# Products of the delta rule's key tiles between the steps of the first projection tile's chain

## The chip, the cores and the metric

The kernel runs on one core of a Trainium2 chip. The metric is the time of one execution in microseconds on the device; before the change it is 2277.63 us, the median of 3 runs (2274.01 to 2280.87).

## What is computed

A trunk of two layers over 512 latent and 256 context tokens of width 1024. In each layer one normalised input goes through one combined input projection into three groups of heads: latent attention (MLA), a bidirectional gated delta rule (GDN) and a bidirectional gated linear attention (GLA). A gated convolutional FFN follows. The part that matters here is the projection and what is made of it for GDN and GLA, shortened from the reference:

```
parts = split(h @ w_in)           # cq, ckv, k_rope, gdn qkv, gate, a, b, gla q, k, v, gate, low rank
k_rope = apply_axial_rope(parts[2])
qkv = silu(dwconv_centred(parts[3], w_conv))       # q, k, v of the delta rule
g = -exp(A_log) * softplus(a + dt_bias); beta = sigmoid(b)
la = logsigmoid(low_rank @ w_gk + b_gk) / 16       # forget gates of GLA, both directions
q, k = l2norm(q), l2norm(k)
o, S = gated_delta_chunked(q, k, v, g, beta, S0)
```

## The kernel before, in words

Activations are kept feature-major: 8 tiles of 128 features by 768 tokens, context first. For accuracy every float32 operand of a projection is split into two fp32r parts, the activations into `hh` and `hl` (`prenorm`, L543 to L550: DVE, ACT and POOL), the weights into `wh` (a cast on ACT, L191) and `wl` (a subtraction on DVE, L192). `wsplit` loads a weight tile with one DMA (L200, into one of 3 `wr` buffers that the conditioning weights of `ada`, L476, use too) and splits its two halves of 4 feature tiles each; there are 3 buffers of `wh` and 3 of `wl`. One projection tile, 128 output features, is 48 products in `fsteps` (L212 through `mm`): 2 segments of 512 and 256 tokens by 8 feature tiles by 3 products (`hh` x `wl`, `hl` x `wh`, `hh` x `wh`), and it yields after each three, 16 times. The result is in a PSUM tile `bb`, of which there are two; smaller PSUM tiles are `a`, `b`, `c` and `d`.

`project_in` runs in each layer right behind the normalisation (in the last layer five kinds of tile come ahead). Its tile 0 holds the small features: the key's rotary part, the low-rank gate inputs, a and b of the delta rule. `misc` makes of them a chain:

- DVE multiplies the tile with the rope table `cse` into `misc` (L584; the table's DMA is L583);
- `selkr` sums the rotary halves on PE, ACT copies the result (L588), a DMA stores `krope` (L589);
- for each of two directions a product with `wgk` into a `bb` tile; DVE makes `m` (L600), ACT makes Abs (L601), Exp (L602) and Ln (L603) of it in `e`, POOL subtracts (L604), and a DMA stores `e` (L606);
- `gdn_gates`: six transposes of `misc` (L215), ACT's softplus and exponentials (L745 to L768), cumulated decays by products with `gg` and `gm`.

`gdn(0)` then makes the two key tiles of the delta rule, `gdn(2)` the two query tiles: each a projection tile, then `conv_silu` (copies `u` out of PSUM, L822, POOL and DVE taps into `cy`, silu on ACT, L808), transposes of `cy` into tokens-major `ktok` (L629), and sums of squares. `self.bg` holds the conditioning products of later stages, `ada`: one piece is issued by `tick` after each projection tile. `gdn_prep` and `gdn_scan` follow, with further projection tiles as their fill.

The code is written as generators. What is issued in the program's order is then ordered anew for each engine by the framework's scheduler, which allots the buffers as well; each engine carries out its instructions in the order that comes of this, and SP's queue issues the DMAs in order.

Of the kernel before, what the change touches and what calls it, by code (L numbers as in the profile page):

```python
# [44 lines left out]
HS, HG, HA, HM, HP = 0, 0, 0, 0, 0  # L45
EP = (1, 1)
WO = ((4, 5, 6, 7, 0, 1, 2, 3), (4, 5, 6, 7, 0, 1, 2, 3))
SPF = 0
XT = (2, 0, 1, 0, 1, 0, 1, 0)
LM = 2  # L50
MOB = 1
HB = 14
NS = 2
# [74 lines left out]
def drain(g):  # L128
    try:
        while True:  # L130
            next(g)
    except StopIteration as e:
        return e.value


class Net:
# [416 lines left out]
    def project_in(self, later):  # L553
# [5 lines left out]
        def fmt(i, segs=XC):  # L559
            wh, wl = self.wsplit(w[i])  # L560
            ps = self.bb()
            yield from self.fsteps(ps, wh, wl, self.hh, self.hl, segs, KT)
            self.tick(1)
            return ps
# [10 lines left out]
        def tok(pool, tag):  # L575
            return pool.tile([128, 6, 256], F32, name=self.nm(tag), tag=tag)

        def misc():

            ps = drain(fmt(0))  # L580
            self.misc = self.kt(name="misc")
            cse = self.kt(name="cse")
            nc.sync.dma_start(cse[:, :T], self.a["rope"][0])  # L583
            nc.vector.tensor_tensor(self.misc[:, :T], ps[:, 256:], cse[:, :T], op=ALU.mult)  # L584
            ps = self.bb()
            for a, b in XC:
                self.mm(ps[:, 256 + a:256 + b], self.c("selkr"), self.misc[:, a:b], True, True)
            nc.scalar.copy(cse[:, :T], ps[:, 256:])  # L588
            nc.sync.dma_start(self.krope, cse[:, :T])  # L589
            if SPF:  # L590
                self.gdn_gates()

            self.spd = []
            for d in range(2):
                ps = self.bb()
                for a, b in XC:
                    self.mm(ps[:, 256 + a:256 + b], self.wgk[:, d * 128:(d + 1) * 128], self.misc[0:32, a:b], True, True)
                e, m = self.kt(name="e")[:, :T], self.kt(name="m")[:, :T]
                bias = self.fm(P_BGK + d)
                nc.vector.tensor_scalar(m, ps[:, 256:], bias, 0.0, op0=ALU.add, op1=ALU.min)  # L600
                nc.scalar.activation(e, ps[:, 256:], AF.Abs, bias=bias)  # L601
                nc.scalar.activation(e, e, AF.Exp, scale=-1.0)  # L602
                nc.scalar.activation(e, e, AF.Ln, bias=1.0)  # L603
                nc.gpsimd.tensor_tensor(e, e, m, op=ALU.subtract)  # L604
                self.spd.append(self.dram([128, T], f"sp{d}"))
                nc.sync.dma_start(self.spd[d], e)  # L606
            if not SPF:
                self.gdn_gates()

        Gp, self.G = self.pool("G", "right")  # L610
        self.ktok, self.vtok, qtok = tok(self.F, "ktok"), tok(self.F, "vtok"), tok(self.G, "qtok")
# [4 lines left out]
        def gdn(m):  # L616
            dst = dsts[m]
            for i in range(2):
                segs = [XS] if (last and m == 2) else XC
                ps = yield from fmt(1 + 2 * m + i, segs)  # L620
                y = self.conv_silu(ps, P_CW + 3 * (2 * m + i), segs)
                for a, b in segs:
                    nt, t0 = (b - a) // 128, a // 128
                    pt = self.ab()
                    for t in range(nt):
                        c = a + t * 128 + (2 if a else 0)
                        self.transpose(pt[:, t * 128:(t + 1) * 128], y[:, c:c + 128])
                    pv = pt[:, :nt * 128].rearrange("p (t c) -> p t c", c=128)
                    nc.scalar.copy(dst[:, t0:t0 + nt, i * 128:(i + 1) * 128], pv)  # L629
                    if m != 1:  # L630
                        sq = self.F2.tile([128, 512], F32, name=self.nm("sq"), tag="sq", bufs=2)
                        sqv = sq[:, :nt * 128]
                        nc.scalar.activation(sqv, pt[:, :nt * 128], AF.Square)
                        nc.vector.reduce_sum(ssv[:, m // 2, t0:t0 + nt, 2 * i:2 * i + 2],
                                             sqv.rearrange("p (t h d) -> p t h d", h=2, d=64), axis=AX)
# [64 lines left out]
        if last:  # L700
            for g in (gdn(2), gate(0), gla_kq(1), mla_in(1)):
                drain(g)
        misc()
        if LM == 0:
            self.bg += later
        drain(gdn(0))
        if LM == 2:
            self.bg += later
        if not last:
            drain(gdn(2))  # L710
        self.tags = "a"
# [854 lines left out]
```

## Time and profile before

| | |
|---|---|
| median of 3 runs | 2277.63 us (2274.01 to 2280.87) |
| the profiled execution | 2278.35 us |
| its span | 2276.6 us |
| mean granted clock of TensorE | 0.934 |
| PE busy | 2045.0 us, 90% of the span |
| DVE, ACT, POOL busy | 1310.4, 1008.7, 536.0 us |
| DMA | 235.64 MB, 30.7% of 16 engines |

PE is matrix products, DVE VectorE, ACT ScalarE, POOL GpSimd, SP the engine that issues most DMAs. The granted clock is a share of TensorE's full 2.4 GHz; 0.5 is 1.2 GHz. A timeline row gives start, duration, engine, line, instruction, and in brackets how long the engine stood idle before it and what ended that. Products of PE overlap, so the distance between two starts is the price of one, not the duration. A row may stand for several instructions of the program: a float32 product counts as two.

### The profile page before, as it was taken

The numbers are of one execution on the slowest core, as the hardware profiler recorded it, in microseconds if no ns is written. First come the engines' busy times: TensorE is split into PE (matmuls) and PEld (weight loads), VectorE is DVE, ScalarE is ACT, GpSimd is POOL, SyncE is SP. The second block draws the span as 40 slices with busy tenths as digits, with TensorE's granted clock in tenths as the row PEclk, the third lists the DMA queues.
The fourth block names the chain that finished last, engine by engine and source line by source line (L and its number), as shares of the span: only waits on it lengthen the run. The fifth ranks groups of instructions, "written<-read, shape, count | busy, mean of one in ns | idle before, by whom it ended". The sixth has DMA issues, their size and how long they took to land. (4 is left out here: it accounts for less than half of the span.)

```text
span 2276.6 us, 44601 instructions
## 1 busy us (share of the span) xinstructions
PE 2045.0 (90%) x18168; PEld 1672.8 (73%) x18168; DVE 1310.4 (58%) x2474; ACT 1008.7 (44%) x1928; POOL 536.0 (24%) x897
## 2 busy tenths in 40 slices
PE   7898999888888799999999969988988777999996
PEld 4677777765667578888888857876766567888886
DVE  3354535668845743354454686556667757655556
ACT  4553323565464633332232456633446446543333
POOL 1342121135502310000010143413122613211102
PEclk8799999998898999999999979999989988999997
DMA  6232345422042354422212333111412053323322
GB/s 262 67 118 100 109 148 164 143 66 68 13 149 92 121 179 167 157 103 65 66 57 66 102 109 124 61 44 62 155 43 96 6 171 102 111 94 96 99 94 92
DMA packets 85134, 235.64 MB, mean 104 GB/s; under 512 B 9088, under 2 KB 24896, under 8 KB 84928
## 3 DMA queue, kind: packets, MB, share of 16 engines
q1 hardware_dynamic: 84928, 232.78, 30.7%
q8 instruction: 143, 2.34, 0.4%
q14 instruction: 63, 0.52, 0.1%
HBM read 204.04 MB, written 28.70 MB: 102 GB/s over the span
## 5 line engine op out<-in xcount | busy, mean ns | idle before, releaser
L212 PE MATMUL bb<-hh,wl 128*128 128x512 f32 (+1 forms) x1520 | 548.3, 361 | 18.0 <-DVE wl L192 10.9
L212 PE MATMUL bb<-hl,wh 128*128 128x512 f32 (+1 forms) x1520 | 542.0, 357 | 5.8 <-POOL hl L550 4.4
L192 DVE TENSOR_TENSOR wl<-wr,wh 128x512 fp32r<-128x512 f32 (+2 forms) x452 | 338.3, 751 | 362.3 <-ACT wh L191 361.0
L212 PE MATMUL bb<-hh,wh 128*128 128x512 f32 (+1 forms) x1520 | 540.2, 355 | 0.0
L191 ACT CAST wh<-wr 128x512 fp32r<-128x512 f32 (+2 forms) x452 | 274.1, 611 | 518.0 <-PE bb L212 370.3
L212 PEld LDWEIGHTS bb<-hh,wl 128*128 128x128 f32 x1520 | 293.2, 193 | 75.2 <-DVE wl L192 14.0
L212 PEld LDWEIGHTS bb<-hl,wh 128*128 128x128 f32 x1520 | 292.8, 193 | 49.4 <-POOL hl L550 7.8
L212 PEld LDWEIGHTS bb<-hh,wh 128*128 128x128 f32 x1520 | 292.9, 193 | 39.6 <-issue 2.1
L212 PE MATMUL bb<-g,wh 128*128 128x512 f32 (+1 forms) x1024 | 263.7, 349 | 2.3 <-DVE g L192 2.3
L1441 POOL TENSOR_SCALAR y<-u,fmt 128x512 f32<-128x512 f32 (+2 forms) x88 | 80.6, 917 | 527.1 <-ACT u L824 525.6
L212 PEld LDWEIGHTS bb<-g,wh 128*128 128x128 f32 x1024 | 181.5, 195 | 27.5 <-DVE g L192 3.3
L212 PE MATMUL bb<-g,wl 128*128 128x512 f32 (+1 forms) x512 | 180.3, 354 | 21.4 <-DVE wl L192 8.5
L212 PEld LDWEIGHTS bb<-g,wl 128*128 128x128 f32 x512 | 99.2, 195 | 36.9 <-ACT g L191 9.3
L824 ACT ACTIVATE u<-bb,fmt 128x512 f32<-128x512 f32 (+1 forms) x118 | 69.0, 613 | 85.0 <-PE bb L212 85.0
L212 PE MATMUL bb<-mh,wl 128*128 128x256 f32 (+1 forms) x256 | 85.2, 333 | 23.4 <-DVE wl L192 15.5
L1468 DVE TENSOR_TENSOR y<-y,bb 128x512 f32<-128x512 f32 (+2 forms) x80 | 54.8, 686 | 82.3 <-PE bb L212 82.2
L505 POOL TENSOR_TENSOR acc<-acc,sq 128x256 f32<-128x256 f32 (+1 forms) x48 | 49.5, 1031 | 183.9 <-ACT sq L503 180.9
L1442 DVE SCALAR_TENSOR_TENSOR y<-u,fmt,y 128x512 f32<-128x512 f32 (+2 forms) x88 | 72.3, 822 | 29.6 <-POOL y L1441 29.6
L212 PE MATMUL bb<-ml,wh 128*128 128x256 f32 (+1 forms) x256 | 84.1, 329 | 0.3
L1380 ACT ACTIVATE P<-bb,ast,srq 128x768 f32<-128x768 f32 (+1 forms) x80 | 72.6, 908 | 23.4 <-DVE ast L1378 14.5
L212 PE MATMUL bb<-mh,wh 128*128 128x256 f32 (+1 forms) x256 | 82.9, 324 | 0.0
L1377 DVE TENSOR_REDUCE ast<-bb 128x1 f32<-128x768 f32 (+1 forms) x80 | 67.2, 842 | 15.9 <-PE bb L212 15.6
(519 smaller groups left out, 3680.4 us busy)
## 6 DMA issues: line engine op xcount, KB each, us to landing
wr<-in_ffn_w_in SPq DMA_DIRECT2D x92, 512.0 KB, 3.5
wr<-in_w_ada SPq DMA_DIRECT2D x80, 512.0 KB, 3.9
wr<-in_ffn_w_out SPq DMA_DIRECT2D x48, 512.0 KB, 3.5
wr<-in_w_in SPq DMA_DIRECT2D x40, 512.0 KB, 4.3
wr<-in_w_out SPq DMA_DIRECT2D x32, 512.0 KB, 3.5
aw<-in_w_ada SPq DMA_DIRECT2D x16, 512.0 KB, 8.5
x<-in_xT SPq DMA_DIRECT2D x16, 384.0 KB, 8.7
wr<-in_w_uq SPq DMA_DIRECT2D x16, 192.0 KB, 2.6
```

The costliest lines, as they stand in the source:

```text
L191: self.nc.scalar.copy(hi, src)
L192: (eng or self.nc.vector).tensor_tensor(lo, src, hi.bitcast(F32), op=ALU.subtract)
L212: self.nc.tensor.matmul(out, l, r, start=start, stop=stop)
L505: (nc.vector, nc.gpsimd)[k % 2].tensor_tensor(acc[k % 2], acc[k % 2], sq, op=ALU.add)
L824: nc.scalar.activation(u[:, a + o:b + o], ps[:, off + a:off + b], AF.Identity, bias=bias)
L1377: nc.vector.reduce_max(st[:, 0:1], sc, axis=AX)
L1380: nc.scalar.activation(P[:, :w], sc, AF.Exp, bias=st[:, 0:1], scale=self.srq[:, t:t + 1], accum_out=st[:, 1:2])
L1441: nc.gpsimd.tensor_scalar(yv, u[:, lo + 1:lo + 1 + n], cw[1], self.fm(P_FCB + i), op0=ALU.mult, op1=ALU.add)
L1442: nc.vector.scalar_tensor_tensor(yv, u[:, lo:lo + n], cw[0], yv, op0=ALU.mult, op1=ALU.add)
L1468: nc.vector.tensor_tensor(y, y, p, op=ALU.add)
```

## The change

`misc` takes the generator of `gdn(0)`, and calls it twice. The first call, between the rope multiply and `selkr`, takes 16 steps: the products of the first key tile. The second, after `krope`'s store, takes 16 more: the rest of the first key tile (convolution, transposes, squares) and the products of the second. What is left of `gdn(0)` is drained after `misc`. The two constants that chose other places for `gdn_gates` and for `self.bg` go, with the places the same as before. Against the lines before, those between the constants and `misc` stand two lower in number (L210 for L212), those in `misc` two or three higher (L603 for L601), those behind it one lower (L807 for L808).

```diff
@@ -45,9 +45,7 @@
 HS, HG, HA, HM, HP = 0, 0, 0, 0, 0
 EP = (1, 1)
 WO = ((4, 5, 6, 7, 0, 1, 2, 3), (4, 5, 6, 7, 0, 1, 2, 3))
-SPF = 0
 XT = (2, 0, 1, 0, 1, 0, 1, 0)
-LM = 2
 MOB = 1
 HB = 14
 NS = 2
@@ -575,20 +573,24 @@
         def tok(pool, tag):
             return pool.tile([128, 6, 256], F32, name=self.nm(tag), tag=tag)
 
-        def misc():
+        def misc(beside):
+
+            def step():
+                for _ in range(16):
+                    next(beside)
 
             ps = drain(fmt(0))
             self.misc = self.kt(name="misc")
             cse = self.kt(name="cse")
             nc.sync.dma_start(cse[:, :T], self.a["rope"][0])
             nc.vector.tensor_tensor(self.misc[:, :T], ps[:, 256:], cse[:, :T], op=ALU.mult)
+            step()
             ps = self.bb()
             for a, b in XC:
                 self.mm(ps[:, 256 + a:256 + b], self.c("selkr"), self.misc[:, a:b], True, True)
             nc.scalar.copy(cse[:, :T], ps[:, 256:])
             nc.sync.dma_start(self.krope, cse[:, :T])
-            if SPF:
-                self.gdn_gates()
+            step()
 
             self.spd = []
             for d in range(2):
@@ -604,8 +606,7 @@
                 nc.gpsimd.tensor_tensor(e, e, m, op=ALU.subtract)
                 self.spd.append(self.dram([128, T], f"sp{d}"))
                 nc.sync.dma_start(self.spd[d], e)
-            if not SPF:
-                self.gdn_gates()
+            self.gdn_gates()
 
         Gp, self.G = self.pool("G", "right")
         self.ktok, self.vtok, qtok = tok(self.F, "ktok"), tok(self.F, "vtok"), tok(self.G, "qtok")
@@ -700,12 +701,10 @@
         if last:
             for g in (gdn(2), gate(0), gla_kq(1), mla_in(1)):
                 drain(g)
-        misc()
-        if LM == 0:
-            self.bg += later
-        drain(gdn(0))
-        if LM == 2:
-            self.bg += later
+        g0 = gdn(0)
+        misc(g0)
+        drain(g0)
+        self.bg += later
         if not last:
             drain(gdn(2))
         self.tags = "a"
```

How the change moves the instructions is shown at three places of layer 0. In the names, a number marks the buffer's turn: before, `bb_471` is the first projection tile, `bb_524` `selkr`, `bb_529` and `bb_541` the two `wgk` products, `bb_638` the first key tile; `a_554` and `b_559` are transposes of `misc`. PE before, from the end of the first tile:

```order
L212 MATMUL bb_471<-hl_93,wh_467 128x256
L212 MATMUL bb_471<-hh_85,wh_467 128x256
L212 MATMUL bb_524<-misc_520,cst 128x512
L212 MATMUL bb_524<-misc_520,cst 128x256
L212 MATMUL bb_529<-misc_520,wgk_212 128x512
L212 MATMUL bb_529<-misc_520,wgk_212 128x256
L215 MATMUL a_554<-cst,misc_520 128x128 x3
L215 MATMUL b_559<-cst,misc_520 128x128 x3
L212 MATMUL bb_541<-misc_520,wgk_212 128x512
L212 MATMUL bb_541<-misc_520,wgk_212 128x256
L212 MATMUL bb_638<-hh_78,wl_631 128x512
L212 MATMUL bb_638<-hl_86,wh_630 128x512
```

PE after the change, at the end of the first tile (`bb_534` is the first key tile, `bb_583` `selkr`, `bb_625` the second key tile):

```order
L210 MATMUL bb_534<-hh_80,wh_526 128x256
L210 MATMUL bb_534<-hh_81,wl_527 128x256
L210 MATMUL bb_471<-hl_93,wh_467 128x256
L210 MATMUL bb_471<-hh_85,wh_467 128x256
L210 MATMUL bb_534<-hl_89,wh_526 128x256
L210 MATMUL bb_534<-hh_81,wh_526 128x256
L210 MATMUL bb_534<-hh_82,wl_531 128x256
```

and further on, to the second key tile:

```order
L210 MATMUL bb_534<-hl_93,wh_530 128x256
L210 MATMUL bb_534<-hh_85,wh_530 128x256
L210 MATMUL bb_583<-misc_520,cst 128x512
L210 MATMUL bb_583<-misc_520,cst 128x256
L213 MATMUL c_699<-cst,misc_520 128x128 x3
L213 MATMUL d_704<-cst,misc_520 128x128 x3
L210 MATMUL bb_625<-hh_78,wl_618 128x512
```

The first key tile's products now stand among those of the first tile, its last 14 between that tile's end and `selkr`, and the second key tile follows the transposes of `misc`. Further on, PE after the change from the end of the second key tile (`bb_674` and `bb_686` are the two `wgk` products, `a_724` and `b_768` products of the gates, `a_863` conditioning products, `bb_810` the first query tile):

```order
L210 MATMUL bb_625<-hh_85,wh_621 128x256
L210 MATMUL bb_674<-misc_520,wgk_212 128x512
L210 MATMUL bb_674<-misc_520,wgk_212 128x256
L210 MATMUL a_724<-gg_711,cst 128x6x4 x2
L210 MATMUL a_724<-gg_711,cst 128x48
L210 MATMUL b_768<-gm_765,ones 64x48 x2
L210 MATMUL a_863<-wr_859,cTs 32x256 x4
L210 MATMUL a_863<-wr_861,cTs 32x256 x4
L210 MATMUL bb_686<-misc_520,wgk_212 128x512
L210 MATMUL bb_686<-misc_520,wgk_212 128x256
L210 MATMUL a_863<-cst,part_872 128x2 x2
L210 MATMUL bb_810<-hh_78,wl_803 128x512
```

Both `wgk` products, which stood ahead of the first key tile, now stand behind the second, with gate and conditioning products between them, and the third projection tile `bb_810` follows. ACT before, from the first table load of the gates (`e_532`, `e_544` are the two directions' gates):

```order
L753 ACT_TABLE_LOAD
L753 ACTIVATE gb_575<-abt_553 128x48
L601 ACTIVATE e_532<-bb_529,fmt_208 128x768
L745 ACTIVATE ge_565<-gz_564 128x48
L602 ACTIVATE e_532<-e_532 128x768
L746 ACTIVATE ge_565<-ge_565 128x48
L603 ACT_TABLE_LOAD
L603 ACTIVATE e_532<-e_532 128x768
L601 ACTIVATE e_544<-bb_541,fmt_208 128x768
L747 ACTIVATE ge_565<-ge_565 128x48
L602 ACT_TABLE_LOAD
L602 ACTIVATE e_544<-e_544 128x768
```

ACT after the change, from the cast of the third tile's second weights (`e_677`, `e_689` the two gates; `wr_904` are weights of the second query tile):

```order
L189 CAST wh_806<-wr_800 128x512
L787 ACTIVATE gl_771<-b_768 128x48
L603 ACTIVATE e_677<-bb_674,fmt_208 128x768
L767 ACTIVATE geg_731<-gc_728 128x48
L766 ACTIVATE gek_730<-gek_730 128x48
L604 ACTIVATE e_677<-e_677 128x768
L189 CAST wh_906<-wr_904 128x512
L481 COPY part_872<-a_863 128x256
L605 ACT_TABLE_LOAD
L605 ACTIVATE e_677<-e_677 128x768
L603 ACTIVATE e_689<-bb_686,fmt_208 128x768
L604 ACT_TABLE_LOAD
```

Between the two Abs stand now two exponentials of the decays, Exp, a weight cast, the copy of `part`, a table load and Ln; before it was Exp, a table load and Ln, with two short steps of the delta rule's gates. By the table loads of the whole program, ACT has 68 before and 72 now. In layer 1 the order has the same form.

## Rows read from the trace of the kernel before

**Rows 1.** The page's first part: busy time, share of the span, instructions.

```profile
PE 2045.0 (90%) x18168; PEld 1672.8 (73%) x18168; DVE 1310.4 (58%) x2474; ACT 1008.7 (44%) x1928; POOL 536.0 (24%) x897
```

**Rows 2.** Windows view, a stretch per layer: start:end, length, each engine's busy time, clock.

```profile
67.00:102.00 35.00, 30.99 (x128) 22.79 (x129) 9.58 (x15) 17.94 (x29) 16.05 (x45) 0.73 0.18 63
...
1409.00:1436.00 27.00, 25.36 (x127) 20.04 (x128) 9.34 (x14) 16.45 (x28) 16.05 (x45) 0.94 0.23 83
```

**Rows 3.** Timeline of PE, layer 0: start, us, instruction, and idle time before it.

```profile
46.67 0.79 PE L212 MATMUL bb<-hh,wl 128*128 128x512 f32 x1 [2.33 <-ACT hh L544]
...
54.79 0.55 PE L212 MATMUL bb<-hh,wh 128*128 128x512 f32 x1
...
62.01 0.58 PE L212 MATMUL bb<-hl,wh 128*128 128x256 f32 x1 [0.84 <-POOL hl L550]
...
66.29 0.41 PE L212 MATMUL bb<-hh,wh 128*128 128x256 f32 x1
...
71.01 2.90 PE L212 MATMUL bb<-misc,cst 128*128 128x512 f32 x4 [4.30 <-DVE misc L584]
...
81.02 0.80 PE L212 MATMUL bb<-hh,wl 128*128 128x512 f32 x1
...
85.45 0.58 PE L212 MATMUL bb<-hl,wh 128*128 128x512 f32 x1
...
92.79 0.40 PE L212 MATMUL bb<-hh,wl 128*128 128x512 f32 x1
...
101.13 0.40 PE L212 MATMUL bb<-hh,wl 128*128 128x512 f32 x1
```

**Rows 4.** Timelines of DVE and of SP's queue, layer 0.

```profile
69.90 0.96 DVE L584 TENSOR_TENSOR misc<-bb,cse 128x768 f32<-128x768 f32 x1 [1.81 <-DMA cse<-in_rope]
...
65.89 0.33 SPq L583 DMA_DIRECT2D cse<-in_rope  x1
```

**Rows 5.** Timeline of PE, layer 0: gate products, transposes of a convolved tile, conditioning products.

```profile
89.06 0.76 PE L212 MATMUL c<-gg,cst 128*128 128x24 f32 x6
...
106.38 0.60 PE L215 MATMUL a<-cst,cy 128*128 128x128 f32 x4
...
110.88 1.07 PE L212 MATMUL a<-wr,cTs 128*32 128x256 f32 x16
```

**Rows 6.** Timeline of ACT, layer 0.

```profile
79.93 0.88 ACT L601 ACTIVATE e<-bb,fmt 128x768 f32<-128x768 f32 x1
...
80.85 0.84 ACT L602 ACTIVATE e<-e 128x768 f32<-128x768 f32 x1
...
81.84 1.28 ACT L603 ACT_TABLE_LOAD   x1
...
83.13 0.84 ACT L603 ACTIVATE e<-e 128x768 f32<-128x768 f32 x1
...
90.62 0.24 ACT L768 ACTIVATE geg<-gc 128x48 f32<-128x48 f32 x1
```

**Rows 7.** The page's group of weight casts: busy, mean ns, idle before; then its DMA part.

```profile
L191 ACT CAST wh<-wr 128x512 fp32r<-128x512 f32 (+2 forms) x452 | 274.1, 611 | 518.0 <-PE bb L212 370.3
...
wr<-in_w_in SPq DMA_DIRECT2D x40, 512.0 KB, 4.3
```

**Rows 8.** Timeline of PE, layer 1.

```profile
1409.49 1.56 PE L212 MATMUL bb<-misc,cst 128*128 128x512 f32 x4 [1.11 <-DVE misc L584]
...
1410.97 1.55 PE L212 MATMUL bb<-misc,wgk 32*128 32x512 f32 x4
...
1412.46 0.55 PE L215 MATMUL b<-cst,misc 128*128 128x128 f32 x3
...
1413.26 1.55 PE L212 MATMUL bb<-misc,wgk 32*128 32x512 f32 x4
...
1415.96 0.50 PE L212 MATMUL bb<-hh,wl 128*128 128x512 f32 x1 [1.15 <-ACT e L601]
...
1435.43 0.40 PE L212 MATMUL bb<-hh,wl 128*128 128x512 f32 x1
```

## The prediction

> **What bounds the kernel now.** The page comes first: PE is busy for 90% of the span [rows 1], so only stretches in which PE waits, or runs at its lower clock, have something to give. The windows view shows one such stretch in each layer, around the chain that follows the first projection tile [rows 2]. In layer 0, from 67 to 102 us, PE is busy for 30.99 of 35 us at a mean granted clock of 0.73; in layer 1, 25.36 of 27 us at 0.94. The timeline of PE then shows where [rows 3]. In layer 0 the last product of the first tile starts at 66.29. PE next stands still for 4.30 us until DVE has made `misc`, runs the chain's small products from 71.01 to 81.02, and begins the first key tile at 81.02 at half clock (1.2 GHz); the full clock (2.4 GHz) is back at 85.45. From 92.79 to 101.13 one whole tile takes 8.34 us without a gap: the price of a tile at full clock. The third tile, the first query tile, starts at 101.13, and at 1435.43 in layer 1 [rows 8]; these two times are my measure of what each layer gains.
>
> What ends last before 71.01 is not PE. DVE starts its multiply at 69.90 after waiting for the rope table, whose DMA SP issues at 65.89 [rows 4]. The change moves neither, so I leave `misc` ready at 70.86 (69.90 plus 0.96).
>
> So layer 0 has 4.30 us of waiting, half of some 10.0 us of chain at half clock, and half of the 4.43 us from 81.02 to 85.45: 4.3 + 5.0 + 2.2 = 11.5 us at most from this place. Layer 1 has waits of 1.11 and 1.15 us [rows 8] and 0.06 of 27 us of clock, 1.6 us: 3.9 us at most.
>
> **The first step.** It issues the first key tile's 48 products after the rope multiply, and the order on PE shows them woven into the first tile's: they fill gaps of the normalisation and end ahead of `selkr`. Two tiles are 16.7 us of products at full clock. From 46.67 [rows 3] the clock is low until 54.79 and high until 62.01. Were that pattern kept with PE never idle, 4.1 + 7.2 us of full-clock work would be done by 62.01, and the remaining 5.4 us at half clock end at 72.8, 1.8 us after 71.01. At full clock after 62.01 they end by 67.4, or shortly after the last normalised tile arrives. I take no delay, as the busier PE leaves fewer gaps such as the 0.84 us ahead of the fall at 62.01, and keep 1.8 us for the range. This tile's weight load and cast are under way in the old program too and cost nothing; their cover is the normalisation.
>
> **The second step.** Behind `selkr` and the gate transposes PE gets the second key tile, with six transposes of the first one inside it; then the first gate product (`wgk`), gate and conditioning products, the second `wgk`, and the third tile. Durations at full clock come from layer 1 [rows 8]: `selkr` 1.48 (1409.49 to 1410.97), `wgk` 1.49 (to 1412.46), transposes of `misc` 0.80 (to 1413.26). Six transposes of a convolved tile are 0.9 us, at 0.60 for four [rows 5]. In layer 0: 71.01 + 1.48 + 0.80 + 8.34 + 0.9 + 1.49 = 84.0 us for the end of the first `wgk`.
>
> **The wait that the change adds.** The second key tile now keeps its PSUM buffer until its convolution, which stands behind the gates. Both `wgk` products and the third tile therefore go one after the other through the other buffer, and each must wait until ACT has read what was in it. On ACT, between the two Abs, stand two small exponentials, Exp, the cast of the next weights, a conditioning copy, a table load and Ln. With the ACT rows [rows 6]: Abs 0.88 ends at 84.9, exponentials (0.24 each) at 85.4, Exp 0.84 at 86.2. The cast waits for its weights: they are issued once the third tile's second weight half is split, which waits for the second key tile's products with its first half to end (about 81, an estimate from the sum above); a cast of 0.61 [rows 7] and a subtraction of similar length bring the issue to about 83, and the 4.3 us of such a load [rows 7] bring them in at 87.4. Then cast 0.61, copy up to 0.5, table load 1.28, Ln 0.84 and Abs 0.88 end at **91.5**, where the third tile starts instead of at 101.13: 9.6 us earlier. Without the wait for the weights it would be 90.3; with weights 2 us later, 93.5. DVE's chain (the `m` of each buffer, and the copies of the gates) runs beside ACT and ends before it. POOL's subtraction and the two stores of `e` on SP hold the weight load behind them until about 97 us; the tile that needs it comes two tiles of 8.34 us after 91.5, so that is covered. SP's stores would show up only if those two tiles were gone.
>
> The second `wgk` ends at 84.9 + 1.49 = 86.4, so PE now idles there for up to 5 us, and the clock may fall. Nearest rows: a wait of 4.30 us left the small products at half clock, and dense work needed from 81.02 to 85.45 to get the full clock back, which costs 2.2 us; in layer 1 the loss was 1.6 us after 1.15 us. I take 2.2, with 0 and 7.2 (low for as long as from 71.01 to 85.45) as bounds.
>
> The third tile also has less behind it: the six transposes (0.9) and eight conditioning products (1.07 [rows 5]) are done. **Layer 0: -9.6 - 0.9 - 1.1 + 2.2 = -9.4 us.**
>
> The table loads are the place where the trace and the notes part. In the rows the Exp and Ln of one gate are 1.28 us of load apart, and nothing more: the load begins at 81.84 and Ln at 83.13 [rows 6]. The Trainium skill (ScalarE: Activation LUTs, What ACT_TABLE_LOAD costs) puts a switch of table set at 1283 ns and a drain of some 1380 ns more, 2.66 us in all. By it one switch between the Abs of each layer would cost 1.4 us more, and the sum would lose 2.8 us; the trace agrees with the load alone, so I keep 1.28.
>
> **Layer 1.** Here the wait for `misc` is short: it began at 1409.49 - 1.11 = 1408.38, and the first key tile now comes first. 1408.4 + 8.34 + 1.48 + 0.80 + 8.34 + 0.9 + 1.49 = 1429.7. On ACT 0.88 + 0.48 + 0.84 + 0.61 + 1.28 + 0.84 + 0.88 = 5.8 us bring the third tile to 1435.5, against 1435.43. The transposes done (-0.9) and the clock after a wait of some 3 us (+1.6, as this layer lost before) leave **+0.8 us**, between -1 and +6.
>
> **The sum** is -8.6 us on the profiled execution of 2278.35 us (2276.6 us of span), 0.7 us above the median of 2277.63: **2269.0 us**. The rest, where the order shifts by a few instructions in many places, I put at nothing, within 4 us either way; the three runs alone lie 6.9 us apart. A measurement tells about 0.3% (6.8 us) from no change.
>
> **Rivals.** (1) *The low clock reaches into the chain.* For it: rows 3 show it low from 62.01 on. The first key tile ends 1.8 us late, `selkr` and the transposes double (+2.3), and the second key tile begins with 4.43 us at half clock (+2.2): +6.3 us, 2275.3. Against it: the idle ahead of the chain shrinks. (2) *Slower: the clock stays low through layer 0's chain and again under layer 1's third tile.* The 13.0 us from `selkr` to `wgk` double, with the 1.8 us: layer 0 ends at +5.4; layer 1 pays 7.2 instead of 1.6, +6.4. Together +11.8, 2289. It decides once half clock costs 8.6 us beyond my sum, about 17 us of dense work at 1.2 GHz; the rows show 23 us low in a row, but only 4.43 of it under dense products, which speaks against. (3) *More.* Full clock throughout and weights in time: the third tile at 90.3, -12.8; layer 1 at -0.8: 2264. The bound of 11.5 us, plus work drawn ahead, allows it only just. (4) *The gain is given back.* Tiles finish earlier, but the stage behind them waits for something with a date of its own: 2277.6. PE at 90% speaks against; two more table loads of ACT in each layer and the stores on SP speak for. (5) *Nothing stands between the steps.* The first step's products lie ahead of the multiply, so part of the 4.30 us stays; this is in the sum, since I left 71.01 in place.
>
> The Trainium skill (TensorE: Matmul & The Clock Gate, HAM oscillation) says that every wait of PE that is long enough lets the clock fall and be paid again; by it a change that trades one wait for another, as this does, keeps the loss. The trace agrees for the wait of 1.15 us in layer 1, after which 1.6 us went; that is rival 2's ground.
>
> **Chances.** My forecast 0.42, (1) 0.18, (2) 0.08, (3) 0.17, (4) with (5) 0.15. With the tails of the first and third, faster has 0.59, same 0.30, slower 0.11. The range of 2258 to 2282 leaves out most of (2) and the low tail of (3).
>
> **What would show it.** Right: in layer 0 the first key tile's products in the normalisation, `selkr` at 71, the third tile at 90 to 93 after a PE wait on ACT's Abs of about 4 us, then products at half clock for some 4 us; in layer 1 the third tile within 1.5 us of 1435.4 counted from its first tile's end. Wrong: `selkr` later than 72, a granted clock of 0.5 under the second key tile, a third tile after 96, or a stage behind the query tiles that grows by what was gained.

## The result, and the profile after

The change made the kernel slower: 2285.68 us (median of 12 runs, 2280.26 to 2298.89) against 2275.61 us for the kernel before (12 runs, 2265.83 to 2281.48). The ratio is 1.0054, with a 95% interval of 1.0039 to 1.0069. Forecast was 2269.0 us. The profiled execution took 2293.36 us, with a span of 2291.6 us and a mean granted clock of 0.929; it is one of the longer of its runs, so its sums exceed the median's. The page's first row of the kernel after:

```profile
PE 2056.9 (90%) x18168; PEld 1683.5 (73%) x18168; DVE 1311.0 (57%) x2474; ACT 1016.5 (44%) x1932; POOL 535.6 (23%) x897
```

PE is busy 11.9 us longer than in [rows 1], so the span's 15 us are only in small part waiting; more of the work runs at half clock, as the mean clock of 0.929 against 0.934 shows.

**The front of layer 0 came out as forecast.** The two executions reach the normalisation at times some 2 us apart, so I count from DVE's multiply with the rope table (at 69.90 before [rows 4]). The timeline of DVE after the change, then that of PE (start, us, instruction, idle before it and what ended that):

```profile
68.14 0.96 DVE L586 TENSOR_TENSOR misc<-bb,cse 128x768 f32<-128x768 f32 x1 [5.58 <-DMA cse<-in_rope]
```

```profile
69.16 1.56 PE L210 MATMUL bb<-misc,cst 128*128 128x512 f32 x4 [0.45 <-DVE misc L586]
...
71.12 0.48 PE L210 MATMUL bb<-hh,wl 128*128 128x512 f32 x1
...
80.30 1.55 PE L210 MATMUL bb<-misc,wgk 32*128 32x512 f32 x4
...
84.90 2.92 PE L210 MATMUL bb<-misc,wgk 32*128 32x512 f32 x4
...
89.86 0.80 PE L210 MATMUL bb<-hh,wl 128*128 128x512 f32 x1 [1.10 <-ACT e L603]
...
100.23 0.40 PE L210 MATMUL bb<-hh,wl 128*128 128x512 f32 x1
...
111.84 0.50 PE L210 MATMUL bb<-hh,wl 128*128 128x512 f32 x1
```

`selkr` starts 0.06 us after the multiply ends, the second key tile at 71.12 at full clock, the first `wgk` at 80.30, the third tile at 89.86: 21.7 us after the multiply, where the forecast had 21.6 and the kernel before 31.2 [rows 3, 4]. The third tile takes 10.37 us (to 100.23) instead of 8.34, 2.0 us more, close to the 2.2 us of half clock that were in the sum. The timeline of ACT shows the chain of the forecast's wait:

```profile
83.05 0.90 ACT L603 ACTIVATE e<-bb,fmt 128x768 f32<-128x768 f32 x1
...
84.10 0.84 ACT L604 ACTIVATE e<-e 128x768 f32<-128x768 f32 x1
...
85.16 0.62 ACT L189 CAST wh<-wr 128x512 fp32r<-128x512 f32 x1 [0.22 <-DMA wr<-in_w_in]
...
86.07 1.28 ACT L605 ACT_TABLE_LOAD   x1
...
87.37 0.84 ACT L605 ACTIVATE e<-e 128x768 f32<-128x768 f32 x1
...
88.91 0.90 ACT L603 ACTIVATE e<-bb,fmt 128x768 f32<-128x768 f32 x1 [0.70 <-DVE m L602]
```

Abs at 83.05, Exp, the cast (its weights are 0.22 us late, not 1.2), the table load of 1.28 us, Ln, and the second Abs at 88.91. The last waited 0.70 us for DVE's `m`, which the forecast had put beside ACT. On PE the time is filled otherwise than forecast: it stands idle for 1.10 us ahead of the third tile, not for up to 5, because the second `wgk` starts 1.8 us later than forecast, counted from the multiply, runs at half clock (2.92 us instead of 1.55), and conditioning products follow it. The table load is followed by Ln 1.30 us after it began, so the drain that the Trainium skill adds (ScalarE: Activation LUTs, What ACT_TABLE_LOAD costs) is not on this path either.

For the fifth tile the kernel before has these rows on PE (layers 0 and 1), and this multiply of layer 1:

```profile
122.52 0.50 PE L212 MATMUL bb<-hh,wl 128*128 128x512 f32 x1
...
1454.28 0.40 PE L212 MATMUL bb<-hh,wl 128*128 128x512 f32 x1
```

```profile
1408.47 0.96 DVE L584 TENSOR_TENSOR misc<-bb,cse 128x768 f32<-128x768 f32 x1
```

From multiply to fifth tile layer 0 took 122.52 - 69.90 = 52.6 us before and 111.84 - 68.14 = 43.7 after: 8.9 us less, forecast 9.4.

**Layer 1's chain cost more than forecast.** Its timelines after the change, of DVE and PE:

```profile
1419.19 0.96 DVE L586 TENSOR_TENSOR misc<-bb,cse 128x768 f32<-128x768 f32 x1
```

```profile
1438.31 1.55 PE L210 MATMUL bb<-misc,wgk 32*128 32x512 f32 x4
...
1442.01 2.71 PE L210 MATMUL bb<-misc,wgk 32*128 32x512 f32 x4 [1.10 <-ACT e L603]
...
1446.77 0.79 PE L210 MATMUL bb<-hh,wl 128*128 128x512 f32 x1 [2.04 <-ACT e L603]
...
1467.58 0.47 PE L210 MATMUL bb<-hh,wl 128*128 128x512 f32 x1
```

PE waits 1.10 and 2.04 us for the two Abs. The third tile comes 27.6 us after the multiply (27.0 before), the fifth 48.4 (45.8 before): +2.6 us, forecast +0.8. At 1720 us, in the table below, 1.4 of it are left (+10.8 at 1380, +12.2).

**The loss lies behind both.** I took the starts of the instructions of DVE, ACT and POOL that both executions have in equal number, and the median shift of those around a time; the table gives that shift in microseconds at times of the kernel before, with 0 at 30 us.

| us of the kernel before | 139 | 301 | 440 | 690 | 860 | 1270 | 1380 | 1436 | 1720 | 2250 |
|---|---|---|---|---|---|---|---|---|---|---|
| after | -10.5 | +2.9 | +10.1 | +8.0 | +5.9 | +5.9 | +10.8 | +15.3 | +12.2 | +14.9 |
| layer 0 alone (first experiment) | -10.6 | +2.0 | +9.2 | +4.6 | +3.6 | +3.6 | +3.9 | +3.9 | +7.9 | +8.4 |

At 139 us the whole gain is there (some 2 us of the -10.5 are none: the thirteenth experiment, which has nothing of the change, stands at -2.0). Then 13.4 us are lost up to 301 and 7.2 up to 440, in the delta rule's preparation and scan, which the change does not touch; layer 0 alone repeats both (12.6 and 7.2). At 1436 the instructions counted are in part ones that the change itself moves: by PE's rows the third tile stands at +11.3 there and the fifth at +13.3. In the profile of run 2 below the stretch from 301 to 860 us, in the order of before, took 6.3 us less than in the profile before, so a difference of that size in one profile, behind 301, says little. The stretch from 1270 to 1380 (+4.9) is left out below: it has the same order and the same work in the kernels compared, and ran as much longer, at half clock, in the thirteenth experiment, which has nothing of the change; I take it for chance of this profile.

**The preparation of layer 0 shows why.** I bound it by two instructions: the first transpose of `ktok` and the first product with the scan's state `Sb`. The windows view of that stretch (start:end, length, PE busy, other engines, clock), layers 0 and 1, before:

```profile
134.84:255.06 120.22, 113.72 (x2441) 88.76 (x2439) 63.49 (x156) 47.97 (x96) 33.56 (x31) 0.97 0.32 111
...
1451.97:1556.29 104.32, 96.28 (x2171) 78.66 (x2169) 59.14 (x133) 45.53 (x92) 27.58 (x26) 0.97 0.16 52
```

and after:

```profile
124.20:254.88 130.68, 117.94 (x2377) 91.73 (x2376) 64.58 (x154) 50.61 (x98) 34.04 (x31) 0.93 0.30 99
...
1467.38:1571.27 103.89, 96.85 (x2218) 79.31 (x2217) 60.11 (x135) 42.16 (x88) 29.35 (x27) 0.93 0.16 50
```

In layer 0 it begins 10.6 us earlier (134.84, 124.20) and ends at the same time (255.06, 254.88): 130.68 instead of 120.22 us for the same work but for 64 small products, which after the change stand behind its end; PE's timeline has 300 projection products of fill in either. PE stands idle for 12.7 instead of 6.5 us (length less busy), and the busy time grows by 4.2 at a clock of 0.93 instead of 0.97. The waits of PE in it (in total, times, longest), before and after:

```profile
PE bb L212 <- DVE wl L192: 1.3, 1, 1.3
PE c L212 <- issue: 0.8, 1, 0.8
PE d L212 <- DVE r L931: 0.8, 1, 0.8
PE a L212 <- DVE modT L486: 0.7, 1, 0.7
```

```profile
PE b L210 <- issue: 3.2, 2, 2.3
PE c L210 <- DVE y L955: 2.6, 1, 2.6
PE a L210 <- ACT part L481: 2.4, 1, 2.4
PE bb L210 <- DVE wl L190: 2.1, 1, 2.1
PE d L210 <- issue: 1.9, 1, 1.9
```

Where most of them stand is seen in PE's timeline. The preparation is a chain of small products (`r`, `s`, `y`, 32 partitions) in which one step needs DVE's or ACT's answer to the one before; fill, above all the projection products `bb<-h..`, covers the waits. Before, the longest stretch without fill lies between these two rows:

```profile
173.14 0.28 PE L212 MATMUL bb<-hh,wl 128*128 128x256 f32 x1
...
187.49 0.39 PE L212 MATMUL bb<-hl,wh 128*128 128x256 f32 x1
```

After, between the first and last of these, with small products between:

```profile
165.27 0.28 PE L210 MATMUL bb<-hh,wl 128*128 128x256 f32 x1
...
169.22 0.99 PE L210 MATMUL b<-r,s 32*32 32x64 f32 x57 [0.85 <-issue]
...
173.11 0.25 PE L210 MATMUL d<-r,s 32*32 32x32 f32 x3 [1.92 <-issue]
...
177.21 0.37 PE L210 MATMUL b<-r,l 32*32 32x32 f32 x11 [2.34 <-issue]
...
180.04 0.58 PE L210 MATMUL bb<-hl,wh 128*128 128x256 f32 x1
```

Both are some 14.5 us long. But added up over the preparation, stretches of over 4 us without fill ("bare" below) are 14.4 us before (this one alone) and 31.1 after (four of them, the longest 14.8). In them lie 2.9 of the 6.5 us of PE's idle time before, and 10.3 of the 12.7 after. The scheduler has placed the same 300 products elsewhere. Seven of the executions have 300 such products in layer 0's preparation: the four with 12.9 to 15.6 us bare (before, runs 2, 4 and 13) took 119.5 to 121.6 us, the three with 30.6 to 39.6 (after, runs 1 and 7) 130.2 to 133.4.

### The profile page after: what moved, and what is told of

The parts are those of the page before. It is cut to its first block, busy times and chain, and to the rows that moved or that the text cites. A ratio compares the mean times of both kernels' runs of the same rounds, so it can differ in the third digit from the quotient of the medians.

```text
span 2291.6 us, 44591 instructions
## 1 busy us (share of the span) xinstructions
PE 2056.9 (90%) x18168; PEld 1683.5 (73%) x18168; DVE 1311.0 (57%) x2474; ACT 1016.5 (44%) x1932; POOL 535.6 (23%) x897
## 3 DMA queue, kind: packets, MB, share of 16 engines
q1 hardware_dynamic: 84928, 232.78, 30.7%
## 5 line engine op out<-in xcount | busy, mean ns | idle before, releaser
L210 PE MATMUL bb<-hh,wl 128*128 128x512 f32 (+1 forms) x1520 | 550.7, 363 | 18.8 <-DVE wl L190 10.2
L210 PE MATMUL bb<-hl,wh 128*128 128x512 f32 (+1 forms) x1520 | 546.3, 360 | 4.7 <-POOL hl L548 3.8
L210 PE MATMUL bb<-hh,wh 128*128 128x512 f32 (+1 forms) x1520 | 542.5, 357 | 0.0
L210 PEld LDWEIGHTS bb<-hh,wl 128*128 128x128 f32 x1520 | 295.7, 195 | 74.1 <-DVE wl L190 13.2
L210 PEld LDWEIGHTS bb<-hl,wh 128*128 128x128 f32 x1520 | 295.4, 194 | 48.1 <-POOL hl L548 6.4
L210 PEld LDWEIGHTS bb<-hh,wh 128*128 128x128 f32 x1520 | 295.3, 194 | 42.4 <-issue 4.2
L210 PE MATMUL bb<-g,wh 128*128 128x512 f32 (+1 forms) x1024 | 265.2, 351 | 2.3 <-DVE g L190 2.3
L210 PEld LDWEIGHTS bb<-g,wh 128*128 128x128 f32 x1024 | 182.6, 196 | 27.8 <-DVE g L190 3.3
L210 PE MATMUL bb<-g,wl 128*128 128x512 f32 (+1 forms) x512 | 181.0, 355 | 21.2 <-DVE wl L190 8.5
L210 PEld LDWEIGHTS bb<-g,wl 128*128 128x128 f32 x512 | 99.6, 195 | 37.0 <-ACT g L189 9.3
L210 PE MATMUL bb<-mh,wl 128*128 128x256 f32 (+1 forms) x256 | 85.1, 333 | 23.7 <-DVE wl L190 14.6
L1467 DVE TENSOR_TENSOR y<-y,bb 128x512 f32<-128x512 f32 (+2 forms) x80 | 54.9, 686 | 83.8 <-PE bb L210 83.7
L210 PE MATMUL bb<-ml,wh 128*128 128x256 f32 (+1 forms) x256 | 84.2, 329 | 0.4
L210 PE MATMUL bb<-mh,wh 128*128 128x256 f32 (+1 forms) x256 | 82.5, 322 | 0.0
```

What stands on the lines that cost most here:

```text
L210: self.nc.tensor.matmul(out, l, r, start=start, stop=stop)
L1467: nc.vector.tensor_tensor(y, y, p, op=ALU.add)
```

## The experiments

Two theories stood against each other first. A: the front gains as forecast, and the time goes in the preparation, through the new order. B: layer 1 carries the loss, and layer 0's later stages are chance. A rival of A came after the first four: the preparation has a date of its own (it ended at 255 in both), and earliness is worth nothing. Times are medians of 12 executions (6 in runs 4 and 7, 9 in runs 8 and 10); the ratio is to the kernel before in the same session (23 to 32 executions, medians from 2272.00 to 2275.95).

| run | us | ratio to before, 95% |
|---|---|---|
| 1 change in layer 0 alone | 2285.59 | 1.0041 (1.0025 to 1.0057) |
| 2 change in layer 1 alone | 2283.98 | 1.0027 (1.0012 to 1.0043) |
| 3 first step alone | 2278.68 | 1.0013 (0.9995 to 1.0031) |
| 4 one step, behind `krope` | 2291.10 | 1.0058 (1.0035 to 1.0081) |
| 5 before, 5 steps of fill | 2280.22 | 1.0023 (1.0006 to 1.0040) |
| 6 change in layer 0, 5 steps | 2270.60 | 0.9990 (0.9974 to 1.0005) |
| 7 second step drains | 2286.73 | 1.0061 (1.0038 to 1.0084) |
| 8 second step behind `wgk` | 2286.70 | 1.0059 (1.0034 to 1.0083) |
| 9 before, 3 steps of fill | 2281.32 | 1.0040 (1.0021 to 1.0060) |
| 10 change in layer 0, 3 steps | 2281.46 | 1.0044 (1.0021 to 1.0068) |
| 11 layer 0, 5 steps there only | 2267.81 | 0.9977 (0.9957 to 0.9997) |
| 12 the same, second step drains | 2268.73 | 0.9979 (0.9961 to 0.9998) |
| 13 before, 16 buffers in a later pool | 2281.27 | 1.0033 (1.0015 to 1.0052) |
| 14 as 11, with 13 buffers | 2264.65 | 0.9961 (0.9945 to 0.9978) |

**1 and 2, one layer at a time.** `step()` does nothing in the other layer:

```diff
-                for _ in range(16):
+                for _ in range(0 if last else 16):     # 1
+                for _ in range(16 if last else 0):     # 2
```

> The change in layer 0 alone; layer 1 keeps the order of before. Theory A (the gain in front of the query tiles is real, 9 to 11 us, and is given back in the preparation of the delta rule, whose products now stand in another order): third tile 9 to 11 us earlier than before, from the third tile to 300 us 12 to 15 us longer than before, and 2 to 7 us slower at the end of layer 0 and in all (2278 to 2283). Theory B (layer 0 gains as forecast, the loss is layer 1's, and what the profile shows in layer 0's later stages is chance): 2264 to 2270.

> The change in layer 1 alone; layer 0 keeps the order of before. Theory A: the chain of layer 1 is 3 to 5 us longer (a wait of PE on ACT's Abs and the half clock behind it), nothing else changes: 2279 to 2281. Theory B: layer 1 carries the whole loss, 2283 to 2290. The sum of the forecast (+0.8): 2276 to 2277.

Layer 0 alone costs 10 us, layer 1 alone 8 (ratios 0.4 and 0.3%). B falls by run 1, 15 us above its range: layer 0 keeps its gain at 139 us and loses it again. A's figures were too small as well: run 1 lies above its 2278 to 2283, run 2 above its 2279 to 2281 and in B's range. Layer 1 alone costs more than its chain: counted from its multiply, 2.4 us up to the fifth tile and some 10 up to 1720, much of that behind the preparation. The windows of the two preparations in run 1, then in run 2:

```profile
124.19:254.39 130.20, 118.17 (x2378) 91.90 (x2376) 64.52 (x154) 50.56 (x98) 34.02 (x31) 0.93 0.30 99
...
1454.64:1568.17 113.53, 101.96 (x2395) 83.47 (x2393) 63.55 (x141) 46.06 (x96) 28.68 (x27) 0.94 0.15 48
```

```profile
131.66:251.17 119.51, 114.33 (x2442) 88.82 (x2440) 62.59 (x156) 48.10 (x96) 33.37 (x31) 0.96 0.33 112
1446.69:1551.93 105.24, 96.98 (x2282) 79.44 (x2280) 61.44 (x136) 42.48 (x89) 29.79 (x27) 0.95 0.16 52
```

In run 1 layer 0 repeats the profile after, with the same order (130.2 us, 30.6 of it without fill). In run 2, with the order of before, it takes 119.5 us and ends at 251.17, earlier than in run 1 (254.39) although it begins 7.5 us later. And there is a surprise that the expectation had wrong: layer 1 of run 1, where nothing is changed, takes 113.53 us instead of 104.32. Its order there is not that of before. Of the 8.4 us that run 1's profile is behind at 2250 us, 3.9 are there ahead of layer 1's preparation and 4.0 come up to 1720.

**3, 4, parts of the change.** In `misc`:

```diff
             nc.sync.dma_start(self.krope, cse[:, :T])
-            step()                                 # 3
...
             nc.vector.tensor_tensor(self.misc[:, :T], ps[:, 256:], cse[:, :T], op=ALU.mult)
-            step()                                 # 4
```

> Only the first key tile stands inside the chain, in both layers; the second comes behind the gates as before. Theory A: the front of layer 0 gains the wait for the rope table and the half clock of the chain, 6 to 10 us, and the preparation behind it gives 5 to 15 back, as its order moves too: 2272 to 2284. Theory B: the waits on ACT's Abs, which only the second step makes, are the loss; without it 2264 to 2270.

> Only one call of 16 steps, between the store of krope and the first wgk product: the first key tile stands there, none ahead of selkr. Theory A: the front gains little (0 to 4 us, since the wait for the rope table and the half clock stay), the preparation is what its order makes it: 2270 to 2284. Theory B: the waits on ACT's Abs come with it: 2278 to 2284.

The first step alone brings the fifth tile of layer 0 3.5 us earlier against the multiply (49.1 us), and delays it by 8.2 in layer 1 (54.0); no difference is left in all (2278.68 lies in A's range). One step behind `krope` makes both layers' third tile later, by 5.7 and 6.3 us against the multiply, where A had a gain of 0 to 4; at 2291.10 it lies above the range of A (to 2284) and of B. Neither tells much about what is behind the front.

**5 and 6, 9 and 10: the fill reshuffled.** `PN` is the number of steps of fill pulled after each small product of the preparation. Each value gives another order behind the front, and a pair has the change in layer 0 or not:

```diff
-PN = 4
+PN = 5        # 5 (before), 6 (layer 0 alone)
+PN = 3        # 9 (before), 10 (layer 0 alone)
```

> The kernel before, with 5 instead of 4 steps of fill between the delta rule's small products: the partner of the next run. No theory speaks of its own time, 2265 to 2290.

> The change in layer 0 alone, with 5 steps of fill. Against its partner the order on PE differs in the front and in some 330 rows up to row 1000, and hardly behind, where the pair with 4 steps differs in some 2,000 rows up to row 2500. Order theory (the front gains 10 us, and what is lost behind it is the new order of the small products and the fill, which another fill reshuffles): 5 to 11 us below its partner. Earliness theory (the preparation has a date of its own, whatever the order: weights, ACT or DVE): within 3 us of its partner or above it, with 10 us or more lost between the third tile and 300 us.

> The kernel before with 3 steps of fill between the delta rule's small products: the partner of the next run, 2265 to 2295.

> The change in layer 0 alone with 3 steps of fill. Its order differs from its partner's in some 2,000 rows of PE, up to row 2900, as with 4 steps. Order theory: the front gains 8 to 11 us against the partner; behind it the time goes either way by up to 13 us, so the whole lies between 11 us below and 6 us above the partner, and what the stretch from the third tile to 300 us loses or gains differs from the 12.6 us of the pair with 4 steps by over 4 us. Earliness theory: that stretch loses 10 to 15 us again.

The preparation of layer 0 in the four (windows view, in the order 5, 6, 9, 10):

```profile
132.87:276.97 144.10, 139.28 (x2775) 109.36 (x2773) 69.16 (x172) 55.75 (x112) 34.44 (x32) 0.95 0.37 123
```

```profile
123.60:265.99 142.39, 137.35 (x2771) 107.46 (x2769) 69.88 (x172) 56.02 (x112) 34.42 (x32) 0.96 0.34 115
```

```profile
129.06:242.13 113.07, 103.71 (x2298) 80.79 (x2296) 61.20 (x149) 49.91 (x96) 34.54 (x35) 0.91 0.30 98
```

```profile
121.80:232.52 110.72, 99.35 (x2342) 77.78 (x2341) 61.12 (x150) 46.64 (x94) 33.50 (x35) 0.95 0.26 89
```

With 5 steps the change is worth 9.6 us (2280.22 to 2270.60; by the two ratios 0.33%, 7.5 us). It begins 9.3 us earlier and now also ends 11.0 us earlier, at 265.99 instead of 276.97, with 13.6 and 10.9 us bare of fill; its order on PE differs there in some 160 of 2,770 products, where the change with 4 steps differs from before in some 640 of 2,400. With 3 steps it ends 9.6 us earlier, at 232.52, but some 16 us are then lost between 300 and 690 us, and nothing is left at the end. So the preparation has no date, and earliness theory falls: with 5 steps both ends lie behind 255, which alone would not exclude a date there, but with 3 steps they lie ahead of it, as do those of runs 2 and 13 with 4 (251.17 and 252.46). The pair with 3 steps also limits the reading by bare fill: the change has more of it there (36.6 against 33.3 us) and more idle (11.4 against 9.4) and is still 2.4 us shorter, at a clock of 0.95 instead of 0.91. Three orders (4, 5 and 3 steps) give nearly the same front and, by the ratios, +9, -8 and +1 us in all.

**7 and 8, the wait for the Abs.** In 7 the second key tile is convolved at once and gives its PSUM buffer back; in 8 the second step comes behind the two `wgk` products:

```diff
             nc.sync.dma_start(self.krope, cse[:, :T])
-            step()
+            drain(beside)                          # 7
...
                 nc.sync.dma_start(self.spd[d], e)
+            step()                                 # 8, and not behind krope
             self.gdn_gates()
```

> The second step runs the generator to its end, so that the second key tile is convolved ahead of the gates and gives its PSUM buffer back before the second wgk product and the third tile need one. Theory of the wait (the buffer costs layer 1 its 4.6 us and layer 0 some 3 us): in layer 1 the stretch from the first tile's end to the third tile is 3 to 5 us shorter than with the change, in layer 0 the third tile comes 2 to 4 us earlier than at 91.8; in all 2275 to 2282. Rival (the table loads and the half clock, which stay): both stretches within 1 us of the change's.

> The second step stands behind the two wgk products and ahead of the transposes for the gates. Theory of the wait: the second wgk product still waits for the Abs of the first, but no cast and no conditioning copy stand between, and the third tile has a free buffer: layer 1's stretch 3 to 5 us shorter than with the change; layer 0's front as early as with the change or 1 to 3 us earlier; in all 2272 to 2284. Rival (table loads, half clock): both stretches within 1 us of the change's.

Without the wait the third tile comes 17.4 us after the multiply in layer 0 (21.7 with the change) and 23.5 in layer 1 (27.6): the wait is real and costs 4 us. At the fifth tile layer 0 keeps 3.2 of them (40.5 us), layer 1 none (48.4, as with the change), and the whole is no faster. In 8 the forecast of the theory is wrong: layer 1's third tile is 6.4 us later than before against the multiply. Both runs lie above the range that the theory had for the whole (2275 to 2282 and 2272 to 2284). The buffer costs something, but is not the loss.

**11 and 12, with before's fill in layer 1.**

```diff
-            self.pace(PN)
+            self.pace(PN if self.last else 5)      # 11, 12
...
-            step()
+            if not last:
+                drain(beside)                      # 12, behind krope
```

> The change in layer 0 alone, with 5 steps of fill in layer 0 and the 4 of before in layer 1. Order theory: layer 0 as in the pair with 5 steps, layer 1 as before, which took 3 us less there: 2264 to 2270, under both kernels. Rival (a pair's gain is chance): 2275 to 2283.

> The same with the second step of layer 0 running the generator to its end, so that the third tile need not wait for the second Abs. The third tile comes 4 to 5 us earlier than with the change; of that 2 to 4 us should be left at the fifth tile. Order theory: the stretch behind, whose order is new again, decides: 2260 to 2282. Theory of the wait (the buffer is what costs): 2260 to 2267.

Both are faster than the kernel before by 0.2%, and so faster than the change. In 11 layer 0 is at 860 us 13.7 us ahead of before; but layer 1's preparation, though nothing is changed there, takes 112.4 us again. In 12, where it has the order of before, it takes 102.2, and layer 0's preparation 148.5 with 34.0 bare. Layer 1's preparation in 11, then in 12:

```profile
1440.90:1553.26 112.36, 102.39 (x2394) 84.00 (x2393) 63.55 (x141) 45.42 (x96) 27.95 (x26) 0.94 0.15 48
```

```profile
1448.66:1550.81 102.15, 94.76 (x2170) 77.70 (x2169) 59.19 (x133) 45.21 (x92) 27.59 (x26) 0.98 0.16 53
```

**13 and 14, the order by itself.** `HB` is a count of buffers in later stages. It was chosen for the order that comes of it: in 13 layer 1 of the kernel *before* has the order of run 1; in 14 layer 1 behind the change has the order of before.

```diff
-HB = 14
+HB = 16       # 13, in the kernel before
+HB = 13       # 14, in run 11
```

> The kernel before with 16 instead of 14 buffers in a pool of the later stages, and nothing of the change. Its order is that of before up to layer 1, but for some 20 rows; in layer 1 it is, row for row on every engine, that of the run with the change in layer 0 alone. Order theory: layer 0 as before, the preparation of layer 1's delta rule 7 to 10 us longer (113 instead of 104 us): 2281 to 2286. Rival (layer 1 was longer by chance, or by what the change leaves behind in layer 0): 2273 to 2278.

> The change in layer 0 alone with 5 steps of fill there, and 13 buffers in that pool, with which layer 1 has the order of before but for 4 rows of PE, and layer 0 the order of the run without this. Order theory: the preparation of layer 1 takes 104 us again instead of 112: 2257 to 2263, under all others. Rival: 2265 to 2271 as without it.

The preparations of layers 0 and 1 in 13:

```profile
132.64:252.46 119.82, 112.82 (x2442) 87.96 (x2440) 63.47 (x156) 47.96 (x96) 33.40 (x31) 0.97 0.32 111
...
1455.05:1566.62 111.57, 100.72 (x2395) 82.40 (x2393) 63.58 (x141) 45.39 (x96) 27.99 (x26) 0.95 0.15 49
```

and in 14:

```profile
126.27:267.88 141.61, 137.22 (x2772) 107.72 (x2770) 69.75 (x172) 55.88 (x112) 34.39 (x32) 0.96 0.35 115
...
1436.74:1541.34 104.60, 96.20 (x2170) 78.72 (x2169) 59.28 (x133) 45.35 (x92) 27.59 (x26) 0.97 0.15 52
```

13 has nothing of the change and loses 0.33% (7.5 us by the ratio): layer 0's preparation is as before (119.8), layer 1's takes 111.57 instead of 104.32, with 26.0 us bare instead of 18.2. That is the order alone. 14 brings it back to 104.60, with 18.8 bare, and has the lowest median of all: 0.9961, 8.9 us by the ratio. Each order of layer 1's preparation thus has three executions: 113.5, 111.6 and 112.4 us in runs 1, 13 and 11, and 104.3, 104.6 and 102.2 before and in runs 14 and 12.

These lengths make the loss too large, though: the longer stretch holds 224 more small products (x2395 against x2171), which in the order of before stand behind its end. By the shifts, from 1436 to 1720 us, runs 13, 1 and 11 lose 4.7, 4.0 and 4.0 us against the profile before, run 14 loses 0.5, and run 12 gains 3.0. So the order costs some 4 to 5 us there. The step from 11 to 14 is 0.16% in the ratios (3.6 us), which is what these shifts give (3.5) but less than the ratios' intervals; the 8 us expected were read from the lengths, and at 2264.65 run 14 lies between the two ranges. The rest of run 13's 7.5 us is not in this stretch.

## Why the prediction was wrong, point by point

- **What bounds the kernel, the first step, the second step:** right. The first key tile cost no time ahead of `selkr`, the chain ran at full clock to the first `wgk`, and rivals (1) and (2) did not come. But the clock fell at 83.8 us, ahead of the wait on the second Abs and not behind it.
- **The wait that the change adds:** right in size and in what ends it, ACT's second Abs (third tile 21.7 us after the multiply, forecast 21.6; with the wait removed in run 7, 4.3 us less). DVE's `m`, said to end before, ended 0.70 us late; the weights came earlier than estimated, 0.22 us after ACT was ready instead of 1.2. Here two errors of the sum nearly cancel.
- **Layer 0: -9.4 us:** measured -8.9 at the fifth tile.
- **Layer 1: +0.8 us:** mis-sized, +2.6 at the fifth tile. The waits for both Abs are there. The third tile is 0.6 us late, close to the forecast; from it to the fifth it takes 2.0 us more, where the sum had +0.7 (1.6 for the clock less 0.9 for the transposes).
- **"The rest, where the order shifts by a few instructions in many places, I put at nothing, within 4 us either way":** this is the step that failed. Forecast was -8.6 us, measured +10.1 (medians); the two fronts account for 2.3 of these 18.7, and some 16 stand in this term. The order on PE differs in over a thousand of some 8,550 rows, and the preparation of layer 0 alone lost 10.5 us. That another order takes or gives several microseconds without the change, runs 13 and 5 show (0.33% and 0.23%). Against the -9.4 us forecast for layer 0, the change in layer 0 came to +9, +1 and -8 us with 4, 3 and 5 steps of fill, so the term was some 18, 10 and 1 us.
- **Rival (4), the gain is given back:** right in that it was, and its sign came, a stage behind the query tiles that grows by what was gained; wrong in its ground. No date of a weight load or a store holds the next stage (with the change in layer 0 it ends anywhere from 232.5 us in run 10 to 269.9 in run 12); the fill stands in other places.

For layer 1 run 13 shows the order's cost without the change. For layer 0 no run has the new order without the change, so there the cause is argued from the pairs and from the executions that repeat an order. Why the scheduler places the fill worse after this change than before is not shown: the order is the outcome of its whole plan, and no run tested its choices one by one. Nor is it shown which instructions behind layer 1's preparation cost run 2 much of its 10 us, nor what makes up the waits that the trace gives as "issue".

## What to carry to other kernels

Where a scheduler orders the program, a change in one stage is two changes: the one that is read from the diff, and a new order in every stage behind it. Price the second from the start: compare the orders past the change, and look where a dependent chain lives on fill from elsewhere. Before a gain is given up, reshuffle the order by a setting that means nothing for the work, with and without the change; the pair tells the change from its order. And when an order moves work across the edge of a stretch, compare times at a point where both orders have done the same work, not the stretch's length.

## What the runs showed of the hardware

- In layer 0 after the change the granted clock fell from 1.0 to 0.5 at 83.8 us. In the 4 us before, PE had waited for 0.46 us at most and had run the end of the second key tile, the first `wgk`, small gate products and the first conditioning products; the second `wgk` then took 2.92 us instead of 1.55. I had expected a fall only behind a wait as long as the 1.15 us of [rows 8].
- From 1270 to 1380 us of the kernel before, all sixteen profiled executions carry out the same instructions in the same order. The clock was at half for 23.9 us of it before and in runs 1, 2, 5, 6, 9, 12 and 14 (which took up to 1.4 us longer than before), for 27.3 us in runs 7, 8 and 11 (2.5 to 2.8 longer), for 30.7 in run 4 (3.6) and for 34.1 after the change and in runs 3, 10 and 13 (4.7 to 5.1).
- From 301 to 860 us run 2 has the order of before but for 10 of 3,940 products, and took 6.3 us less, with 93 us at half clock instead of 109.
